# A 512-wide gate projection, weights outermost, in a two-layer hybrid block on one core

## The chip, the core and the metric

The kernel runs on one core of one Trainium2 chip. The metric is the device time of one execution in microseconds (us). The engines are named as in the profile: PE (matmuls; PEld are its weight loads), DVE (vector), ACT (activations and copies), POOL, and SP, whose queue here only issues DMAs. Each engine works through its own instruction list strictly in order, so an instruction that waits holds everything behind it on that engine.

## The reference

Two layers over 512 latent tokens (of width 1024) and 256 context tokens. Cut to what matters here:

```
for i in range(DEPTH):                       # 2 layers
    ctx_out = i < DEPTH - 1                  # the last layer gives no context output
    h  = rms_norm(x,  w) * (1 + sc_m)  + sh_m
    hc = rms_norm(cx, w) * (1 + csc_m) + csh_m
    ua, ub, ug = jnp.split(h @ w_in[i], splits, axis=-1)     # NA | SSD | GQA
    ...
    ya = neighbourhood_attention(...); yb = ssd_mixer(...); yg = gqa_attention(...)
    x = x + g_m * (concat([ya, yb, yg]) @ w_out[i])
    x = x + g_f * swiglu(...)

# in ssd_mixer: ub holds z (512 columns), xbc (1024 columns) and dt
z, xbc, dt_raw = jnp.split(v, [SSD_WIDTH, SSD_WIDTH + SSD_CONV_CH], axis=-1)
xbc = silu(depthwise_conv(xbc, conv_w, conv_b))
...
y = (y_f + flip(y_b) + d_skip * xs) * silu(z)                # the gate
y = rms_norm(y, norm_w)
```

The change concerns only `z`, the 512 columns of the input projection that gate the SSD output.

## The kernel before

Products are made from two parts, a rounded high part and a remainder, so each block of 128 rows of a projection takes three matmuls (high by high, high by low, low by high). Normed activations lie in SBUF as eight tiles of 128 features by 768 tokens, high parts `hh` and low parts `hl` (the names HY, HS, HZ, PHA, PHB in the profile). Tokens are counted in blocks of 128: `ntt` is 6 in layer 0 (latent and context) and 4 in layer 1 (latent only).

A layer runs through: norm, NA projections and attention, GQA projections, the eight blocks b of the SSD's `xbc` (projection on PE, a copy out of PSUM on ACT at L758 and L761, the convolution as a chain on DVE at L763 and L768, the tanh on ACT at L772, the product on DVE at L774), the decays of the SSD (L850: small products of `dA`; L852: ACT copies one to an SA tile, from which DMAs write `crow`), the z projection, and then the GQA or NA attention with the SSD core woven in between. The attention is cut into units: `scores` (PE L390 and L393 into a PSUM tile S, DVE L398 to L403 for the maximum, ACT L410 for the exponential, tile pr), then a scaling on POOL (L415), transposes (PE L424 into PSUM tiles PT, copies at L428 and L430) and the product with the values (PE L436). The SSD core's `diag` takes a chunk of tokens and four heads: it loads rows of `crow` into tiles wh and wl (L884, on SP's queue), then ACT L888 (four instructions), DVE L892 (four), ACT L894, a small matmul L897, DVE L899 and L900 into tiles SA and SB, POOL L903 into a tile MA, and DVE L907 and L908.

PSUM has three kinds of tile, two buffers of each: S of 1024 columns (two banks), PT and sm of 512 columns (one bank). In SBUF there are two buffers of SA (256 columns), two of MA (776 columns), two of `wr` for raw weights and three each of `wh` and `wl`, which `load_w` fills (DMA, ACT copy at L326, DVE subtraction at L327) and in which `diag` keeps its tiles too.

In the z projection `p_z(g)` works on one half g of the columns at a time. Two weight tiles, of four k each, are loaded; for each block of tokens 24 matmuls of 128x256 (in `proj_as`, activations stationary) fill one PT or sm tile, which is then read by ACT (L805, a tanh into an SA tile) and DVE (L806), and a DMA on ACT's queue (L807) writes the SA tile to a DRAM tile `zsp[g]`. `load_z` (L991, SP's queue) reads it back later into HZ tiles. The calls that come last put `scores(0)` and `scores(1)` of the first units between the last blocks of tokens.

The order of each engine is set once, when the kernel is built: a scheduler reads the program and fixes the lists. A tile's next user waits until every reader of the buffer before it is done.

## Time and profile before

| | |
|---|---|
| median of three runs | 1846.74 us (1846.3 to 1852.83) |
| profiled execution, span from first to last instruction | 1843.3 us |
| mean granted TensorE clock in it | 0.973 of full speed |
| PE busy | 1737.0 us (94%) |
| DVE, ACT, POOL busy | 1104.0 us (60%), 681.5 us (37%), 423.1 us (23%) |
| z projection in layer 0, first to last matmul | 258.36 us to 301 us of the span |
| z projection in layer 1 | 1265.53 us to 1291 us |

The profiled execution has no time of its own beside its span; the median of the runs lies 3.4 us above the span, and what lies around the first and the last instruction is in that difference. A share of busy time is a mean over stages; what ends last at a place is read from the waits and from the rows around it.

### The profile page before, as it was taken

Reading aid. Unit: us, or ns where it says so; the run is one execution under the profiler, and the core shown is the slowest. Engines: PE = TensorE matmul, PEld = TensorE weight load, DVE = VectorE, ACT = ScalarE, POOL = GpSimd, SP = SyncE. Lnnn points to the kernel's source line nnn. Section 1 sums busy time; section 2 is a strip of 40 time slices with the busy share of each in tenths; the row PEclk is TensorE's granted clock in tenths of the full one; section 3 lists DMA queues with packets and bytes.
Section 4 is the critical chain, followed back from the end, with each engine's and each line's share of the span. In section 5 each row is a group of like instructions: output and inputs, shape, how many; then the busy total and the mean of one; then the engine's idle time right before and its main releaser. Section 6 shows DMA issues by size and latency. Waiting matters only on the chain.

```text
span 1843.3 us, 26677 instructions
## 1 busy us (share of the span) xinstructions
PE 1737.0 (94%) x10146; PEld 1478.4 (80%) x10146; DVE 1104.0 (60%) x2209; ACT 681.5 (37%) x1386; POOL 423.1 (23%) x429
## 2 busy tenths in 40 slices
PE   7987778989999999999999999999899999999998
PEld 3887667777878888888888887989677788888887
DVE  4559996877475555455654576587786743333334
ACT  5554555556344221121112224334555442232222
POOL 0488886654010000000000002241653100000000
PEclk9998889989989999999999999999999999999999
DMA  9542526433123334333443454342631323333332
GB/s 368 201 139 103 163 89 186 140 90 106 56 75 115 114 115 126 103 116 107 124 129 102 130 163 139 96 131 79 183 105 53 108 90 93 99 96 92 103 100 83
DMA packets 94319, 221.66 MB, mean 120 GB/s; under 512 B 18416, under 2 KB 26224, under 8 KB 94192
## 3 DMA queue, kind: packets, MB, share of 16 engines
q1 hardware_dynamic: 78096, 204.65, 35.6%
q10 hardware_dynamic: 16096, 15.31, 2.5%
q8 instruction: 80, 1.31, 0.3%
q14 instruction: 47, 0.39, 0.1%
HBM read 198.49 MB, written 21.43 MB: 119 GB/s over the span
## 4 chain that ended last, share of the span: by engine, by line
PE 76%; DVE 11%; DMA 5%; ACT 3%; issue 2%; POOL 2%; SPq 0%; ACTq 0%; DVEq 0%; POOLq 0%
PE S L338 61%; PE sm L436 3%; DVE MB L768 2%; DMA wl<-crow 2%; PE PT L424 2%; DVE wl L327 1%; PE PT L338 1%; PE PT L352 1%; PE sm L352 1%; DMA wr<-in_mod_wT_dram 1%; DVE wh L892 1%; PE S L390 1%; ACT wh L326 1%; PE sm L913 1%; PE sm L914 1%
## 5 line engine op out<-in xcount | busy, mean ns | idle before, releaser
L326 ACT ACTIVATE wh<-wr 128x1024 fp32r<-128x1024 f32 (+3 forms) x214 | 207.6, 972 | 732.2 <-PE S L338 542.4
L327 DVE TENSOR_TENSOR wl<-wr,wh 128x1024 fp32r<-128x1024 f32 (+3 forms) x214 | 250.0, 1169 | 174.0 <-ACT wh L326 171.6
L269 POOL TENSOR_TENSOR tiny<-tiny,mhalf 128x2 f32<-128x2 f32 (+2 forms) x17 | 28.7, 1688 | 1067.5 <-DVE tiny L1160 1020.3
L338 PE MATMUL S<-HY,wh 128*128 128x512 f32 (+1 forms) x716 | 214.0, 357 | 5.9 <-ACT HY L318 4.1
L338 PE MATMUL S<-HY,wl 128*128 128x512 f32 (+1 forms) x716 | 214.5, 357 | 0.0
L338 PE MATMUL S<-HZ,wh 128*128 128x512 f32 (+1 forms) x716 | 212.8, 355 | 0.8 <-DVE HZ L319 0.8
L338 PE MATMUL S<-HS,wl 128*128 128x512 f32 (+1 forms) x716 | 213.1, 355 | 0.0
L338 PE MATMUL S<-HS,wh 128*128 128x512 f32 (+1 forms) x716 | 211.1, 353 | 0.0
L231 DVE CUSTOM_DVE_ANT_0 PT<-wr,XFB 128x512 f32<-128x512 f32 x112 | 75.5, 715 | 179.8 <-DMA wr<-in_mod_wT_dram 179.8
L338 PEld LDWEIGHTS S<-HY,wh 128*128 128x128 f32 x716 | 119.8, 192 | 27.2 <-ACT HY L318 4.4
L338 PEld LDWEIGHTS S<-HZ,wh 128*128 128x128 f32 x716 | 118.2, 191 | 21.7 <-DVE HZ L319 2.2
L338 PEld LDWEIGHTS S<-HS,wh 128*128 128x128 f32 x716 | 118.8, 191 | 20.2
L338 PEld LDWEIGHTS S<-HY,wl 128*128 128x128 f32 x716 | 118.8, 191 | 18.8
L338 PEld LDWEIGHTS S<-HS,wl 128*128 128x128 f32 x716 | 118.0, 190 | 18.6
L338 PE MATMUL S<-PHA,wh 128*128 128x512 f32 (+1 forms) x358 | 106.4, 355 | 0.0
L338 PE MATMUL S<-PHB,wh 128*128 128x512 f32 (+1 forms) x358 | 105.0, 351 | 0.0
L338 PE MATMUL S<-GX,wh 128*128 128x512 f32 (+1 forms) x400 | 97.2, 349 | 0.4 <-DVE KA L1114 0.4
L415 POOL TENSOR_SCALAR pr<-pr,tiny 128x640 f32<-128x640 f32 (+2 forms) x80 | 69.3, 869 | 84.0 <-DVE tiny L414 64.3
L768 DVE SCALAR_TENSOR_TENSOR MB<-MA,c,MB 128x770 f32<-128x770 f32 (+1 forms) x64 | 85.3, 1333 | 1.4
L228 POOL TENSOR_TENSOR KA<-QN,XFB 128x512 f32<-128x512 f32 x48 | 73.9, 1546 | 44.3 <-ACT XFB L205 23.5
L424 PE MATMUL PT<-c,pr 128*128 128x128 f32 x384 | 66.5, 289 | 13.4 <-POOL pr L415 4.6
L1261 DVE TENSOR_TENSOR MB<-S,MA 128x768 f32<-128x768 f32 (+1 forms) x42 | 34.6, 823 | 72.6 <-PE S L338 72.5
(402 smaller groups left out, 3911.7 us busy)
## 6 DMA issues: line engine op xcount, KB each, us to landing
wr<-in_mod_wT_dram SPq DMA_DIRECT2D x56, 512.0 KB, 3.7
wr<-in_w_gate_dram SPq DMA_DIRECT2D x44, 512.0 KB, 3.5
wr<-in_w_up_dram SPq DMA_DIRECT2D x44, 512.0 KB, 3.5
wr<-in_w_blk_dram SPq DMA_DIRECT2D x28, 512.0 KB, 3.6
wr<-in_w_down_dram SPq DMA_DIRECT2D x32, 448.0 KB, 3.3
QN<-in_mod_wT_dram SPq DMA_DIRECT2D x48, 256.0 KB, 3.3
wr<-in_w_out_dram SPq DMA_DIRECT2D x32, 256.0 KB, 2.6
wr<-in_w_down_dram SPq DMA_DIRECT2D x16, 512.0 KB, 3.4
```

The lines of the kernel that those rows point to most:

```text
L228: G.tensor_tensor(out=p_, in0=wv, in1=x, op=ALU.mult)
L231: V.tensor_tensor_reduce(out=p_, in0=wv, in1=x, scale=1.0, scalar=0.0, op0=ALU.mult, op1=ALU.add, accum_out=acc[:, o : o + 1],)
L269: POW.tensor_tensor(out=y, in0=v, in1=mhalf[:, 0:n], op=ALU.pow)
L326: S.activation(hi, raw, AF.Copy)
L327: V.tensor_tensor(lo, raw, hi.bitcast(F32), ALU.subtract)
L338: ins = PE.matmul(pt[:, c0:c1], lhsT=w, rhs=xx[:, c0:c1], start=(k == (0 if len(order) == 1 else order[0]) and i == 0), stop=(k == (nk - 1 ...
L352: PE.matmul(pt[:, 0:n], lhsT=s, rhs=w[:, o : o + n], start=(k == 0 and i == 0), stop=(k == KB - 1 and i == 2),)
L415: G.tensor_scalar(out=p_, in0=p_, scalar1=m[:, 4:5], scalar2=1.0, op0=ALU.mult, op1=ALU.mult)
L424: PE.transpose(pt[:, k * P : (k + 1) * P], pr[j, qi][:, kk * P : (kk + 1) * P], ident)
L436: PE.matmul(pv[64 * j : 64 * j + 64, 0:P], lhsT=V2(kts[k], j), rhs=ph[j, qi][:, k, :], start=(k == 0), stop=(k == nkt - 1), tile_position= ...
L768: V.scalar_tensor_tensor(ac[:, 0:wid], cp[:, j : j + wid], convw[l][:, b, j : j + 1], ac[:, 0:wid], ALU.mult, ALU.add)
L1261: V.tensor_tensor(gg[:, c0:c1], pu[:, c0:c1], sg[:, c0:c1], ALU.mult)
```

## The change

`p_z` no longer takes a half at a time. It takes a PSUM bank of 512 columns for every block of tokens at once: the two S tiles give four banks in layer 0 (in layer 1 one S tile gives two), and the last two blocks take the two PT tiles. The weights are regrouped: each of the four loads holds two k of all 512 columns. One load after the other passes by all blocks of tokens: six matmuls of 128x512 for each block and load, with `start` at the first k and `stop` at the last. Only in the fourth pass does a bank become complete; then ACT (L819) writes the tanh of 512 columns into an MA tile (before: 256 columns into SA), DVE (L820) makes the product and a DMA on ACT's queue (L821) writes it to the one DRAM tile `zsp`. `load_z` reads 256 of 512 columns of it, for three blocks of tokens at a time.

In numbers: 288 matmuls of 128x256 in layer 0 become 144 of 128x512, and 192 become 96 in layer 1. The tanh, the product and the DMA are issued 10 times instead of 20. The weight loads stay four in each layer, of the same size. Lines after the edit stand 14 lower than before (L888 becomes L902, L894 L908, L899 L913, L907 L921, L884 L898).

```
-        zsp = [dr.tile([P, 6, 256], F32, name=nm("zsp"), tag=nm("zsp")) for _ in range(2)]
-
-        def p_z(g):
-            wz = [load_w(a["w_z"][l, g, i].rearrange("p k c -> p (k c)"), 1024) for i in range(2)]
-            for t in range(ntt):
-                yield
-                pt = ps_sm() if t % 2 else ps_t()
-                proj_as(pt, wz, 256, 4, hh, hl, t)
-                th = sa()
-                S.activation(th, pt[:, 0:256], AF.Tanh, scale=0.5)
-                V.scalar_tensor_tensor(th, th, 1.0, pt[:, 0:256], ALU.add, ALU.mult)
-                nc.scalar.dma_start(zsp[g][:, t, :], th)
+        zsp = dr.tile([P, 6, 512], F32, name=nm("zsp"), tag=nm("zsp"))
+
+        def p_z():
+            pz = []
+            for t in range(0, ntt - 2, 2):
+                pt = ps_s()
+                pz += [pt[:, 0:512], pt[:, 512:1024]]
+            pz += [ps_t(), ps_t()]
+            for i in range(4):
+                wh, wl = load_w(a["w_z"][l, i].rearrange("p k c -> p (k c)"), 1024)
+                for t in range(ntt):
+                    yield
+                    for k in range(2 * i, 2 * i + 2):
+                        o = slice((k % 2) * 512, (k % 2) * 512 + 512)
+                        h0, l0 = (z[k][:, t * P : (t + 1) * P] for z in (hh, hl))
+                        for j, (s_, w) in enumerate(((h0, wh), (h0, wl), (l0, wh))):
+                            PE.matmul(
+                                pz[t], lhsT=s_, rhs=w[:, o],
+                                start=(k == 0 and j == 0), stop=(k == KB - 1 and j == 2),
+                            )
+                    if i == 3:
+                        th = ma([P, 512])
+                        S.activation(th, pz[t], AF.Tanh, scale=0.5)
+                        V.scalar_tensor_tensor(th, th, 1.0, pz[t], ALU.add, ALU.mult)
+                        nc.scalar.dma_start(zsp[:, t, :], th)
...
-                    nc.sync.dma_start(t[:, 0:n, :], zsp[g][:, 3 * i : 3 * i + n, :])
+                    nc.sync.dma_start(t[:, 0:n, :], zsp[:, 3 * i : 3 * i + n, 256 * g : 256 * g + 256])
...
-        for n, _ in enumerate(z for g in range(2) for z in p_z(g)):
-            if n == 2 * ntt - 2:
+        for n, _ in enumerate(p_z()):
+            if n == 4 * ntt - 2:
                 scores(0)
-            if n == 2 * ntt - 1:
+            if n == 4 * ntt - 1:
                 scores(1)
...
-    r["w_z"] = c(np.stack([act(wi[:, :, 768:1024]), act(wi[:, :, 1024:1280])], 1))
+    r["w_z"] = c(wi[:, :, 768:1280].reshape(2, 4, 2, 128, 512).transpose(0, 1, 3, 2, 4))
```

Three places show how the lists of the engines move. The first is PE's list at the end of z in layer 0, before: the last block of tokens (sm_2924) stands right ahead of `scores(2)`, the third unit.

```order
L352 MATMUL sm_2924<-wh_2729,HS_424 128x256
L352 MATMUL sm_2924<-wl_2730,HS_424 128x256
L352 MATMUL sm_2924<-wh_2729,PHB_432 128x256
L390 MATMUL S_2977<-KA_2861,QN_2858 128x384
L393 MATMUL S_2977<-KA_2861,QN_2858 128x256
L390 MATMUL S_2977<-KB_2864,QN_2858 128x384
L393 MATMUL S_2977<-KB_2864,QN_2858 128x256
L424 MATMUL PT_2999<-c_66,pr_2880 128x128 x3
```

The same place in the changed kernel: S_2534 holds blocks 0 and 1 of z, S_2535 blocks 2 and 3; S_2728 and S_2753 are the tiles of `scores(0)` and `scores(1)`.

```order
L813 MATMUL S_2534<-wl_2667,HS_424 128x512
L813 MATMUL S_2534<-wh_2666,PHB_432 128x512
L390 MATMUL S_2728<-KA_2713,QN_2710 128x384
L393 MATMUL S_2728<-KA_2713,QN_2710 128x256
L390 MATMUL S_2728<-KB_2716,QN_2710 128x384
L393 MATMUL S_2728<-KB_2716,QN_2710 128x256
L813 MATMUL S_2535<-wh_2666,HS_423 128x512
...
L813 MATMUL S_2535<-wh_2666,PHB_432 128x512
L390 MATMUL S_2753<-KA_2713,QN_2710 128x384
```

The scores now stand between the last blocks of z in the same two buffers of S: the first takes the buffer of blocks 0 and 1, the second that of blocks 2 and 3, so each has to wait until both of its banks have been read out.

The second place is ACT's list there, before: the tanh of a 256-wide block (L805), its DMA (L807) and the exponentials (L410) of the first two units alternate.

```order
L410 ACTIVATE pr_2880,tiny_2872<-S_2867,tiny_2872 128x640
L805 ACTIVATE SA_2907<-PT_2882 128x256
L807 DMA zsp_1197<-SA_2907 128x256
L410 ACTIVATE pr_2920,tiny_2916<-S_2911,tiny_2916 128x640
L805 ACTIVATE SA_2949<-sm_2924 128x256
```

In the changed kernel, from the eviction of block 0 (MA_2676) to the second exponential (pr_2762):

```order
L819 ACTIVATE MA_2676<-S_2534 128x512
L902 ACTIVATE wl_2921<-wl_2921,dtr_2519 128x128 x4
L821 DMA zsp_1196<-MA_2676 128x512
...
L819 ACTIVATE MA_2686<-S_2534 128x512
L819 ACTIVATE MA_2696<-S_2535 128x512
...
L819 ACTIVATE MA_2706<-S_2535 128x512
L410 ACTIVATE pr_2741,tiny_2733<-S_2728,tiny_2733 128x640
...
L819 ACTIVATE MA_2772<-PT_2537 128x512
L908 ACTIVATE wh_3058<-wh_3058 128x512
L410 ACTIVATE pr_2762,tiny_2758<-S_2753,tiny_2758 128x640
```

All six evictions now stand in a row through two buffers of MA, so each of them from the third on waits for the DMA of the one two before; the second exponential stands behind the sixth, and four instructions of `diag` (L902) stand between the first eviction and its DMA.

The third place is PE's list at the end of z in layer 1, where S_11573 holds blocks 0 and 1, and the other S buffer is free for the units; S_11778 is the tile of `scores(2)`. Before, `scores(2)` stood behind the last z matmul:

```order
L352 MATMUL sm_12024<-wl_11888,HS_10206 128x256
L352 MATMUL sm_12024<-wh_11887,PHB_10214 128x256
L390 MATMUL S_12073<-KA_11961,QN_11958 128x384
L393 MATMUL S_12073<-KA_11961,QN_11958 128x256
L390 MATMUL S_12073<-KB_11964,QN_11958 128x384
```

Now block 1 of z stands behind it:

```order
L813 MATMUL PT_11575<-wh_11668,PHB_10037 128x512
L390 MATMUL S_11778<-KA_11704,QN_11701 128x384
...
L393 MATMUL S_11778<-KB_11707,QN_11701 128x256
L813 MATMUL S_11573<-wh_11668,HS_10028 128x512
...
L813 MATMUL S_11573<-wh_11668,PHB_10037 128x512
L390 MATMUL S_11812<-KA_11704,QN_11701 128x384
```

The first two `scores` have moved up into the z projection there, the third stands before its last six matmuls.

## Rows read from the trace of the kernel before

**Rows 1.** The page, chain that ended last, share of the span by engine.

```profile
PE 76%; DVE 11%; DMA 5%; ACT 3%; issue 2%; POOL 2%; SPq 0%; ACTq 0%; DVEq 0%; POOLq 0%
```

**Rows 2.** Waits of PE, 258 to 330 us: in total, times, longest.

```profile
PE S L390 <- ACT pr L410: 6.5, 2, 6.2
PE PT L352 <- ACT SA L852: 4.3, 1, 4.3
```

**Rows 3.** Windows: PE, PEld, DVE, ACT, POOL busy; granted clock, DMA share, GB/s.

```profile
258.00:280.00 22.00, 17.73 (x127) 17.49 (x126) 19.98 (x19) 10.10 (x27) 18.95 (x13) 0.84 0.26 83
...
300.00:320.00 20.00, 11.77 (x62) 9.59 (x60) 15.84 (x45) 10.18 (x28) 15.63 (x22) 0.83 0.65 204
```

**Rows 4.** Timeline of PE, layer 0: start, duration, [idle before <- releaser].

```profile
258.36 0.28 PE L352 MATMUL sm<-wh,HY 128*128 128x256 f32 x1
...
264.42 0.28 PE L352 MATMUL sm<-wh,PHB 128*128 128x256 f32 x1
268.97 0.58 PE L352 MATMUL PT<-wh,HY 128*128 128x256 f32 x1 [4.27 <-ACT SA L852]
269.35 0.42 PE L352 MATMUL PT<-wl,HY 128*128 128x256 f32 x1
...
274.26 0.41 PE L352 MATMUL sm<-wh,HY 128*128 128x256 f32 x1
```

**Rows 5.** Timeline of ACT, layer 0, around the first stall.

```profile
265.50 0.84 ACT L772 ACTIVATE MA<-MB 128x770 f32<-128x770 f32 x1 [8.52 <-DVE MB L768]
...
268.28 0.37 ACT L761 ACTIVATE MA<-S 128x256 f32<-128x256 f32 x1
268.55 0.37 ACT L852 ACTIVATE SA<-PT 96x256 f32<-96x256 f32 x1
```

**Rows 6.** Timeline of PE, layer 0: `scores(2)` after z, and `scores(4)` after the second stall.

```profile
301.48 0.34 PE L390 MATMUL S<-KA,QN 128*128 128x384 f32 x1
...
310.47 0.69 PE L390 MATMUL S<-KA,QN 128*128 128x384 f32 x1 [6.20 <-ACT pr L410]
```

**Rows 7.** Timeline of DVE, layer 0, in the second stall.

```profile
307.19 0.29 DVE L899 TENSOR_TENSOR SA<-sm,c 128x128 f32<-128x128 f32 x1 [2.66 <-DMA zsp<-SA]
...
308.40 0.97 DVE L907 TENSOR_TENSOR wl<-wh,SB 128x512 f32<-128x512 f32 x1
...
309.75 0.67 DVE L908 TENSOR_TENSOR wh<-wh,SA 128x512 f32<-128x512 f32 x1
```

**Rows 8.** Timeline of SP's queue, layer 0, around the loads of z.

```profile
299.15 1.95 SPq L991 DMA_DIRECT2D HZ<-zsp  x3
...
307.17 0.33 SPq L884 DMA_DIRECT2D wh<-crow  x1
```

**Rows 9.** Waits of PE, 1265 to 1320 us.

```profile
PE S L390 <- ACT pr L410: 3.1, 2, 2.0
```

**Rows 10.** Timeline of PE, layer 1: a block of z, 24 matmuls, then scores.

```profile
1284.45 0.28 PE L352 MATMUL PT<-wh,HY 128*128 128x256 f32 x1
...
1287.33 0.34 PE L390 MATMUL S<-KA,QN 128*128 128x384 f32 x1
```

**Rows 11.** Timeline of PE, layer 1: 512-wide matmuls, six from the first to the last.

```profile
1255.51 0.40 PE L338 MATMUL S<-HZ,wh 128*128 128x512 f32 x1
...
1256.88 0.39 PE L338 MATMUL S<-PHA,wh 128*128 128x512 f32 x1
```

**Rows 12.** Timeline of ACT, layer 0: an exponential and the four instructions of diag.

```profile
309.53 0.79 ACT L410 ACTIVATE pr<-S,tiny 128x640 f32<-128x640 f32 x1 [5.88 <-DVE tiny L403]
...
310.32 1.27 ACT L888 ACTIVATE wl<-wl,dtr 128x128 f32<-128x128 f32 x4
```

**Rows 13.** Groups of DVE, 258 to 500 us: count | busy, mean ns of one.

```profile
L774 DVE SCALAR_TENSOR_TENSOR GC<-MA,MB 128x512 f32<-128x512 f32 x2 | 1.5, 744 | 1.4 <-ACT MA L772 1.4
```

**Rows 14.** Line L807, the DMA of z.

```profile
DMA to landing us min/median/max: 1.7/3.0/6.2
```

**Rows 15.** The page, DMA issues: count, KB each, us to landing.

```profile
wl<-crow SPq DMA_DIRECT2D x20, 256.0 KB, 4.0
```

## The prediction

> **What bounds the kernel now.** I read the chain that ended last first: three quarters of it are PE's own work, the rest is other engines and DMAs on which PE waited [rows 1]. So a change pays in two ways: by fewer PE cycles where PE runs without a gap, or by a shorter wait where it stands still. The table of PE's waits around the z projection of layer 0 shows where it stands still: two stalls, one of 4.3 us inside z and one of 6.2 us right behind it [rows 2]. The windows show what each stall costs beyond itself: the granted clock of the 20 us windows around them is 0.84 and 0.83 [rows 3]. The timeline has the same in single rows: after the first stall the 256-wide matmuls start 0.213 us apart (23 of them from 269.35 to 274.26) [rows 4], where they start 0.120 us apart in layer 1 (24 in 2.88 us) [rows 10]; that is 1.2 in place of 2.4 GHz, and 26 matmuls at 0.093 us more make 2.4 us.
>
> The first stall comes from ACT's queue. The next z matmul needs the PT buffer that the copy L852 reads; L852 stands behind a tanh of the convolution that waited 8.52 us for DVE's chain and began at 265.50, and behind the copies of the last `xbc` block, L761 among them [rows 5]. The second stall is longer: `scores(2)` ran right behind the last z matmul at 301.48, `scores(3)` passed too, and `scores(4)` at 310.47 waits for an exponential [rows 6], which itself sat behind a maximum on DVE, and DVE's queue stood at L899, whose SA buffer a z DMA was still reading [rows 7]. SP's queue was held too: it stood at the loads of z until 299.15, and the `crow` rows of the second and third `diag` could only be issued behind them, the last of these at 307.17 [rows 8]. In layer 1 the z projection has no stall of this kind; behind it PE waits 3.1 us in two pieces for exponentials [rows 9].
>
> **What the change does to PE's own time.** A 512-wide matmul takes 0.228 us from start to start (six in 1.37 us) [rows 11], two 256-wide ones 0.240 [rows 10]. Both are at the full clock and each has a weight load of its own, so the pair's saving is 0.012 us: 144 pairs in layer 0 make 1.7 us, 96 in layer 1 make 1.2 us, together **-2.9 us**. The bounds: none, if a 512-wide z matmul costs what two of 256 do, and -4 if the rounding of the rows (0.005 us a pair) falls the other way.
>
> The Trainium skill ("TensorE: Matmul & The Clock Gate", section "Wait — 56ns, not 53.3ns?") states a fixed cost of about 2.5 ns per matmul at the full clock on top of its columns. By that page alone a pair would give back 2.5 ns and the 240 pairs an estimated 0.6 us; the rows show 12 ns and are taken.
>
> **The first stall.** PE now does 30 matmuls of 512 (6.8 us) and the two small `dA` products (0.2 us) after its start at 258.36 before it needs something that is not free: the second S buffer, which ACT's L761 releases at 268.28 + 0.37 = 268.65. It stops at 265.4 and goes on at about 268.8, so it waits 3.4 us in place of 4.3: **-0.9 us**. The slow clock behind it stays, as the stop is of nearly the same length. Bounds: 0, if L852's copy, still one step later in ACT's list, is what is waited for, and -4.3 - 2.4 if ACT gets there early, for which nothing speaks, since the tanh that it waits for is DVE's and not touched. The first three passes have 78 matmuls left by then: 268.8 + 78 x 0.228 + 2.4 for the slow clock puts the start of the last pass at W = 289.0, and its 36 matmuls could end at 297.2 if nothing held them.
>
> **The end of z in layer 0.** This is the place where the change adds waits. Durations: tanh of 512 columns 0.6 (between a copy of 256 columns, 0.37 [rows 5], and an exponential of 640, 0.79 [rows 12]); product of 512 columns on DVE 0.74 [rows 13]; landing of a z DMA 3.0, at most 6.2 [rows 14]; `crow` rows 4.0 [rows 15]; the four ACT instructions of `diag` 1.27 [rows 12].
> - Block 0 is complete early in the pass. Its DMA on ACT's queue is behind `diag`'s four instructions, whose rows are loaded into a weight buffer that comes free at W: W + 0.5 + 4.0 + 1.3 = W + 5.8. It lands at W + 8.8 and frees the first MA buffer.
> - Block 1 is multiplied in order after blocks 0, 2, 4 and 5 and ends at W + 7.2. DVE reaches its product after work of `diag` at about W + 9.3 and is done at W + 10. `scores(0)` needs both banks of that buffer: it starts at W + 10.1, 2.9 us late.
> - Block 3 ends at W + 12.1. Its tanh waits for the DMA of block 1 (W + 13), the product ends at W + 14.4, and `scores(1)` starts there, 2.3 us late.
> - Block 5's tanh waits for the DMA of block 3: issued at W + 15, landed at W + 18. The second exponential stands behind it and ends at W + 20. So `scores(3)` runs at W + 20.2 = 309.2 and `scores(4)`, which needs the third exponential, at 310.0 to 311.
>
> Before, `scores(4)` ran at 310.47 [rows 6]. The 1.7 + 0.9 = 2.6 us by which z could end earlier are therefore eaten at this point: **+2.6 us**. Bounds: a single landing at 6.2 in place of 3.0 adds 3.2; if the `crow` rows come early, as their buffer is free in the pass before, 3 are saved.
>
> What comes back later: the `crow` rows of the second and third `diag` now stand ahead of the loads of z on SP's queue, and L899 no longer waits for a z DMA, since SA isn't used. The DVE work of `diag` which fell into the second stall and right behind it (L899, L907 and L908, 0.29 + 0.97 + 0.67 [rows 7], and some 1.5 that I reckon for L900 and L892 beside them) is done while PE waits for its evictions. That is some 3.4 us of DVE time out of the stretch in which each exponential waits for DVE. I take two thirds of it, **-2.2 us**, between 0 (another engine is late next: ACT, with as many instructions as before) and -3.4.
>
> **Layer 1.** Here one S buffer stays free, `scores(0)` and `scores(1)` move up into z, and the exponential of the first is done early. What is lost: `scores(2)` and then block 1 of z wait for exponential and eviction, and the second half of the units begins later by up to 4 us; what is gained are the two units that run under z. I take **0** between -3 and +3; PE's waits there are 3.1 us now [rows 9], so no more than that is to be had.
>
> **ACT and DVE counts.** 10 tanh of 512 in place of 20 of 256 save ACT 20 x 0.37 - 10 x 0.6 = 1.4 us [rows 5, 12], DVE saves something of the kind, and ten DMAs fewer are issued on ACT's queue. Both engines are half idle, so this counts at nothing. The loads of z read runs of 256 columns in place of whole rows; they are needed by the gate many units later, which hides them.
>
> **The sum.** -2.9 - 0.9 + 2.6 - 2.2 + 0 = -3.4 us. Against the profiled execution's span of 1843.3 that is 1839.9, and with the 3.4 us that lie between that span and the median, **1843**.
>
> **The rivals.**
> - *Nothing comes out* (a pair of 256 costs no more than one of 512, or what PE gains is waited away in both layers and stays away): -2.9 and -2.2 fall out, or the waits take them: 1845 to 1848. For it: `scores(4)` is at the same place by my own walk. Against: the rows on 512-wide matmuls.
> - *The second stall goes.* If the evictions keep pace (landings near 1.7 [rows 14], `crow` rows early), exponential two comes by 304, and PE neither stops for 6.2 us [rows 2] nor runs on at 1.2 GHz behind it. The clock of 0.83 over 20 us [rows 3] and a pause like that of the first stall put the slow piece at 2 to 2.5 us. -2.9 - 0.9 - 6.2 - 2.2 = -12: 1835. For it: the wait on SA is gone by construction. Against: the chain of three DMA round trips through two MA buffers.
> - *The banks are held* (slower). All S and both PT are full until the very end, and nothing can run on PE while ACT and DVE read them out. If the landings are at 6.2 twice in the chain of blocks 1, 3 and 5, `scores(4)` comes 6.4 us later; PE then has three stops in a row and starts each time at 1.2 GHz, some 2.4 us each for two of them [rows 4], and in layer 1, where block 1 and both PT banks are held in the same way, the bound of +3 is reached: -3.4 + 6.4 + 4.8 + 3 = +10.8, which is 1857.5. The point from which it decides: `scores(4)` later than some 316 in the new trace. The Trainium skill speaks for this side: "Perfetto Trace Analysis", section "Matmuls" under "Optimizing Tensor Performance", wants independent groups to rotate through different banks so that the read-out of one lies beside the matmuls of the next, and in the same place calls larger matmuls more efficient. The trace agrees with the first half: while z rotates through PT and sm in layer 1, no matmul of it waits. Against its weight here: only the last pass reads out, and PE has 36 matmuls to do meanwhile.
>
> **How the numbers follow.** The sum's case 0.52, with a range of its own of 1838 to 1848 from the bounds above; nothing comes out 0.19; the second stall goes 0.16; the banks are held 0.13. What a measurement of this kernel tells from no change is about 0.5%, 9.2 us. Only the third case is faster than that, with a little of the first: 0.17; only the fourth is slower: 0.13; the same 0.70. The range of 8 in 10 takes the first two cases whole and the near parts of the others: 1834 to 1854.
>
> **What the new profile would show.** z matmuls 0.228 us apart in both layers; the first stall at 265.4 for some 3.4 us, released by an ACT copy; a wait of 2 to 3 us ahead of `scores(0)` and of `scores(1)` in layer 0, named by DVE's product; the second exponential near 308 and behind L819; L899 without a wait for a z DMA; in layer 1 a wait ahead of `scores(2)`. Wrong I would be by the length of the eviction chain above all: by where the `diag` rows land on ACT's queue, and by what DVE does between the products.

## The result and the profile after

The changed kernel took **1861.32 us** in the median of four runs (1859.58 to 1864.02), the kernel before 1846.52 beside it on the same chip (1841.97 to 1852.83): a ratio of **1.0083, 95% interval 1.0065 to 1.0100**. It is slower by 15 us, outside the range of 1834 to 1854; the rival "the banks are held", 1857.5, came nearest. The profiled execution has a span of 1860.7 us and took 1862.52, so 1.8 us lie around a span and not 3.4; the mean granted clock is 0.965.

From the page of the changed kernel, the busy time of each engine, and the chain that ended last by engine (answers to [rows 1]):

```profile
PE 1743.2 (94%) x9906; PEld 1471.8 (79%) x9906; DVE 1102.2 (59%) x2199; ACT 681.8 (37%) x1376; POOL 419.3 (23%) x429
...
PE 77%; DVE 11%; DMA 7%; ACT 2%; issue 2%; POOL 1%; SPq 0%; ACTq 0%; DVEq 0%; POOLq 0%
```

PE is busy 6.2 us longer than before, though each z matmul is cheaper, and DMA has 7% of the chain in place of 5%. The waits of PE in layer 0 from 258 to 330 us (answers to [rows 2]):

```profile
PE S L813 <- ACT MA L761: 4.1, 1, 4.1
PE S L390 <- ACT pr L410: 4.1, 2, 2.6
PE S L390 <- DVE MA L820: 3.6, 1, 3.6
PE S L813 <- DVE MA L820: 2.0, 1, 2.0
PE PT L424 <- ACT PHA L428: 1.7, 1, 1.7
PE PT L424 <- POOL pr L415: 1.3, 1, 1.3
```

These are seven stops of 16.8 us in all. The one of 6.2 us is gone as one piece; waits for read-outs (DVE's L820), exponentials and copies stand in its place. The windows of the changed kernel (answers to [rows 3], and one in layer 1):

```profile
258.00:280.00 22.00, 17.91 (x72) 14.36 (x71) 17.82 (x15) 10.96 (x27) 14.71 (x11) 0.92 0.25 76
300.00:320.00 20.00, 11.53 (x41) 8.72 (x42) 11.26 (x35) 8.61 (x21) 6.37 (x9) 0.71 0.54 178
1305.00:1325.00 20.00, 14.24 (x60) 10.67 (x62) 13.58 (x34) 10.09 (x23) 9.61 (x12) 0.66 0.52 158
```

Around the first stall the clock is better than before, 0.92 for 0.84. Behind z it is worse, 0.71 for 0.83, with 41 matmuls in 20 us. The timeline of PE in the changed kernel, layer 0 (answers to [rows 4, 6]):

```profile
263.04 0.39 PE L813 MATMUL S<-wh,HZ 128*128 128x512 f32 x1
267.52 0.80 PE L813 MATMUL S<-wh,HY 128*128 128x512 f32 x1 [4.09 <-ACT MA L761]
...
271.88 0.39 PE L813 MATMUL PT<-wh,HY 128*128 128x512 f32 x1
...
286.84 0.39 PE L813 MATMUL S<-wh,HS 128*128 128x512 f32 x1
...
294.69 0.80 PE L813 MATMUL S<-wh,HS 128*128 128x512 f32 x1 [2.02 <-DVE MA L820]
...
301.24 0.48 PE L390 MATMUL S<-KA,QN 128*128 128x384 f32 x1 [3.63 <-DVE MA L820]
...
306.49 0.45 PE L390 MATMUL S<-KA,QN 128*128 128x384 f32 x1 [1.46 <-ACT pr L410]
...
313.42 0.69 PE L390 MATMUL S<-KA,QN 128*128 128x384 f32 x1 [2.59 <-ACT pr L410]
...
314.65 0.52 PE L390 MATMUL S<-KA,QN 128*128 128x384 f32 x1
...
317.22 1.33 PE L424 MATMUL PT<-c,pr 128*128 128x128 f32 x5 [1.30 <-POOL pr L415]
...
321.33 0.69 PE L390 MATMUL S<-KA,QN 128*128 128x384 f32 x1
```

The 66 matmuls from 271.88 to 286.84 are 0.227 us apart, as forecast, and the first stall has the releaser that it was given; it begins at 263.4 for a forecast of 265.4. The last pass began at W = 286.84. From there on all is later than the forecast: `scores(0)` (301.24) at W + 14.4 for W + 10.1, `scores(1)` (306.49) at W + 19.7 for W + 14.4, `scores(3)` (313.42) at W + 26.6 for W + 20.2. The stop at 294.69 had no place in the prediction at all: block 1 of z, in the second half of the S tile, waits until DVE has read block 0 out of the first half. The two pieces of SP's queue and of ACT's that set these times in the changed kernel:

```profile
286.80 5.81 SPq L358 DMA_DIRECT2D QN<-nq  x4
292.70 0.54 SPq L898 DMA_DIRECT2D wl<-crow  x1
...
304.63 0.32 SPq L898 DMA_DIRECT2D wl<-crow  x1
...
308.26 7.65 SPq L597 DMA_DIRECT2D GR<-in_rpb_dram  x3
```

```profile
296.86 0.40 ACT L902 ACTIVATE wl<-wl,dtr 128x128 f32<-128x128 f32 x1 [2.95 <-DMA wl<-crow]
296.87 0.33 ACTq L821 DMA_DIRECT2D zsp<-MA  x1
...
305.07 0.60 ACT L819 ACTIVATE MA<-S 128x512 f32<-128x512 f32 x1 [4.69 <-PE S L813]
...
311.32 0.60 ACT L819 ACTIVATE MA<-PT 128x512 f32<-128x512 f32 x1 [1.34 <-DMA zsp<-MA]
```

The `crow` rows of the second `diag` were not issued at W + 0.5 but at W + 5.9, behind four loads of `QN` that held SP's queue for 5.8 us. ACT therefore reached `diag`'s four instructions at 296.86, and the first DMA of z behind them left at W + 10.0 for W + 5.8. The rows of the third `diag` left at 304.63, behind z's last matmuls, whose weights are in the buffers that they go to; the `GR` rows stand behind them. POOL, in the changed kernel:

```profile
313.73 1.19 POOL L917 TENSOR_TENSOR MA<-GX,dtv 128x256 f32<-128x256 f32 x2 [6.19 <-DMA zsp<-MA]
...
316.37 1.57 POOL L415 TENSOR_SCALAR pr<-pr,tiny 128x640 f32<-128x640 f32 x2
```

The wait of L899 on SA [rows 7] is gone, as forecast. It has come back on MA: POOL's product for `diag` (L917) waits 6.2 us for a z DMA, and the scaling of the second exponential (L415) stands behind it. The transposes at 317.22 and `scores(5)` at 321.33 follow. In layer 1 the first two of these stops of PE were foreseen, the last two not (answers to [rows 9]):

```profile
1305.61 0.69 PE L390 MATMUL S<-KA,QN 128*128 128x384 f32 x1 [2.88 <-ACT pr L410]
...
1307.55 0.79 PE L813 MATMUL S<-wh,HS 128*128 128x512 f32 x1 [0.50 <-DVE MA L820]
...
1315.75 0.69 PE L424 MATMUL PT<-c,pr 128*128 128x128 f32 x2 [2.12 <-ACT PHA L428]
...
1318.88 0.87 PE L424 MATMUL PT<-c,pr 128*128 128x128 f32 x3 [1.82 <-DVE PHA L430]
```

**Where in the program the time lies.** I took three marks from the timeline of PE: z's first matmul, the last P V matmul (L436) of the layer, and z's first matmul of the next layer. From z to the last P V the profiled executions took

| | layer 0 | layer 1 |
|---|---|---|
| before, before again (e11), the old z beside a changed other layer (e2, e1) | 211.1, 210.4, 216.4 | 154.0, 153.7, 151.5 |
| after, after again (e5), the changed z in this layer alone (e1, e2) | 222.4, 219.4, 219.9 | 157.2, 160.1, 153.6 |

so the means are 8 us apart in layer 0 and 4 in layer 1, the single pairs 3 to 12 and 0 to 9. In layer 0 the three of a row have the same lists on PE, ACT and DVE, so the same lists spread over up to 6 us there from one execution to the next, and two single profiles do not show a smaller difference. Between the layers, from the last P V of layer 0 to z of layer 1, the changed kernel took 5.1 us more than before in its first profile and none more in e5: that was one execution's. Behind the last P V of layer 1 PE's remainder is 419 to 421 us in every profile. Inside layer 0, two pieces: the 60 us from z's start, and what follows. The changed kernel's windows for both, the second whole and then its first 100 us in three (the count behind PE's busy time is matmuls):

```profile
256.00:316.00 60.00, 44.42 (x179) 34.88 (x177) 38.34 (x61) 25.42 (x63) 33.54 (x34) 0.88 0.44 138
316.00:478.40 162.40, 148.60 (x1089) 119.27 (x1089) 117.50 (x333) 94.66 (x264) 88.45 (x113) 0.93 0.38 110
316.00:356.00 40.00, 35.32 (x246) 28.48 (x246) 23.51 (x72) 19.93 (x55) 25.96 (x33) 0.84 0.60 170
356.00:396.00 40.00, 34.83 (x255) 27.92 (x257) 32.89 (x96) 22.83 (x68) 25.08 (x34) 0.96 0.42 115
396.00:416.00 20.00, 17.70 (x112) 14.33 (x113) 15.99 (x43) 13.16 (x35) 8.50 (x11) 0.83 0.19 61
```

and the same two pieces, uncut, of the kernel before profiled again (e11), with a window of the feed-forward part as a third row, for the last section:

```profile
257.10:317.10 60.00, 48.11 (x346) 45.43 (x345) 42.65 (x76) 28.22 (x75) 43.59 (x42) 0.89 0.56 171
317.10:467.50 150.40, 138.07 (x1068) 111.30 (x1066) 114.96 (x325) 91.42 (x258) 81.94 (x105) 0.98 0.37 106
500.00:1000.00 500.00, 495.30 (x2852) 436.21 (x2851) 275.84 (x579) 119.73 (x145) 8.56 (x8) 0.99 0.37 113
```

A wide z matmul counts for two narrow ones, so the 346 of before are 202 of after (144 fewer); the changed kernel has done 179. The 23 that it lacks are, at before's 150.4 / 1068 = 0.141 us each, an estimated 3.2 us. The rest of the 12 us between these two profiles, 8.8 us, arises behind these 60 us (5 to 9 us over the pairs of before, e11, after and e5): the clock is 0.84, 0.96 and 0.83 in the next 100 us, and 0.98 over all that is left of the layer in e11. Part of this can come without the change: in e2, whose layer 0 is that of before, the same two pieces are

```profile
259.50:319.50 60.00, 45.59 (x336) 43.90 (x334) 39.51 (x70) 25.71 (x69) 39.92 (x39) 0.89 0.54 165
319.50:475.90 156.40, 142.71 (x1078) 114.66 (x1076) 118.74 (x331) 94.07 (x266) 84.79 (x108) 0.96 0.35 104
```

with 10 matmuls fewer than e11 in the first and 6.0 us more in the second.

### The profile page after: what moved, and what is told of

It is laid out like the page before. It is cut to its first block, busy times and chain, and to the rows that moved or that the text cites. A ratio compares the mean times of both kernels' runs of the same rounds, so it can differ in the third digit from the quotient of the medians.

```text
span 1860.7 us, 26142 instructions
## 1 busy us (share of the span) xinstructions
PE 1743.2 (94%) x9906; PEld 1471.8 (79%) x9906; DVE 1102.2 (59%) x2199; ACT 681.8 (37%) x1376; POOL 419.3 (23%) x429
## 4 chain that ended last, share of the span: by engine, by line
PE 77%; DVE 11%; DMA 7%; ACT 2%; issue 2%; POOL 1%; SPq 0%; ACTq 0%; DVEq 0%; POOLq 0%
PE S L338 59%; DMA wl<-crow 3%; PE sm L436 3%; DMA wr<-in_mod_wT_dram 2%; PE PT L424 2%; DVE MB L768 2%; DVE wl L327 2%; PE S L813 2%; PE PT L352 1%; PE PT L338 1%; PE S L390 1%; PE PT L813 1%; PE sm L352 1%; PE sm L927 1%; PE sm L928 1%
## 5 line engine op out<-in xcount | busy, mean ns | idle before, releaser
L326 ACT ACTIVATE wh<-wr 128x1024 fp32r<-128x1024 f32 (+3 forms) x214 | 207.7, 972 | 732.5 <-PE S L338 558.2
L415 POOL TENSOR_SCALAR pr<-pr,tiny 128x640 f32<-128x640 f32 (+2 forms) x80 | 68.3, 858 | 98.9 <-DVE tiny L414 77.4
```

What stands on the lines that cost most here:

```text
L326: S.activation(hi, raw, AF.Copy)
L415: G.tensor_scalar(out=p_, in0=p_, scalar1=m[:, 4:5], scalar2=1.0, op0=ALU.mult, op1=ALU.mult)
```

## The experiments

All ratios are to the kernel before, run in the same call, with 95% intervals. "L0" and "L1" are the two stretches of the table above. Diffs are against the changed kernel where nothing else is said. A profile is of one execution: those of e2, e4, e5 and e7 are of the longest of the kernel's runs, those of e3 and e16 of the shortest.

The lists are fixed anew for each kernel, so an edit also moves instructions that it does not name. I compared the order in the traces, from z's start to the last P V of layer 0 and without z's own instructions. Of 387 on DVE and 1121 on PE, so many stand outside the longest order that a kernel shares with the changed one:

| | DVE | PE |
|---|---|---|
| e7, e9 | 18, 25 | 29, 17 |
| before, e4, e8, e13 | 30, 30, 36, 41 | 24, 20, 41, 47 |
| e3 and e12, e6 and e14 | 95, 104 | 140, 142 |
| e16, e18 | 129, 148 | 257, 311 |

So the kernels of the last two rows differ from the changed one by another order as well as by their edit, and what they show is of both together.

**e1, e2: one layer alone.** The wide projection in one layer, the two halves of 256 in the other.

```diff
-        for n, _ in enumerate(p_z()):
+        wide = l in (0,)          # e2: (1,)
+        for n, _ in enumerate(p_z() if wide else (z for g in range(2) for z in p_zg(g))):
```

> The changed z projection in layer 0 alone, the old one in layer 1. Before 1846.5 us, changed kernel 1861.3. In the profile of the changed kernel the ACT weight copies run 1.2 us ahead of those of before when z of layer 0 begins, 8.9 late when its attention ends, 13 to 14 late in layer 1's start, 17.3 late at the end. If layer 0's z costs the 10 us and the steps of 5 us in between belong to the execution and not to the change: 1856 to 1858. If the 5 us follow the change in layer 0: 1860 to 1862. If both layers carry the loss alike: 1853 to 1855.

> The changed z projection in layer 1 alone. By the same reading of the ACT copies layer 1's z and attention lose 3.2 us: 1849 to 1851. If the loss of 5 us at the start of layer 1 belongs to the changed program of layer 1: 1853 to 1856. If layer 1 gains what its matmuls save: 1844 to 1846.

Layer 0 alone: 1852.61 us, 1.0030 [1.0018, 1.0042], L0 219.9. Layer 1 alone: 1845.49 us, 1.0001 [0.9978, 1.0024], L1 153.6, no longer than before. So layer 0 carries the loss, but the two parts, 7 and 0 us, do not add to the 13 to 15 of both: the 3 to 6 us of layer 1 only show where layer 0 is changed too. That stays open. The layer 0 of e2, which is that of before, is the 216.4 of the table.

**e3, e12: the width undone.** The same passes and the same banks, each 512 as two of 256 (`start` with the first half, `stop` with the second).

```diff
-  PE.matmul(pz[t], lhsT=s_, rhs=w[:, o], start=..., stop=...)
+  for q in (0, 256):
+      PE.matmul(pz[t][:, q : q + 256], lhsT=s_, rhs=w[:, o][:, q : q + 256], start=..., stop=...)
```

> The changed kernel with each 512-wide z matmul as two of 256 into the same bank; weights outermost, banks, evictions and order of passes as changed. If the waits at the end of z carry the loss and the width only the -2.9 us that the rows gave: 1862 to 1865. If the width itself is what costs: 1847 to 1852. If the width gains nothing because the end of z is set by waits on DMAs that do not move: 1861 again.

> The kernel with each z matmul as two of 256 once more, a second profile. In the first one layer 0's feed-forward part, which no edit touches, took 580.5 us where all other kernels take 589 to 590. If that belongs to the program, it shows again and the kernel's 1846.2 hides a loss of some 9 us in the attention; if it was one execution's, the part takes 589 to 590.

1846.20 us, 1.0003 [0.9988, 1.0018]: with dearer matmuls the loss is gone (e12 is one profiled execution, 1852.13). L0 is 214.9 and 212.3. By the time alone that is the case "the width itself is what costs", but 95 of 387 DVE instructions stand elsewhere too, so the width is not shown to be the cause. The timeline of PE in e3 shows that block 1 no longer stops:

```profile
297.74 0.50 PE L814 MATMUL S<-wh,HS 128*128 128x256 f32 x2
...
301.24 0.41 PE L390 MATMUL S<-KA,QN 128*128 128x384 f32 x1 [1.22 <-issue]
```

PE comes to block 1 at 297.74 without a stop, and `scores(0)` runs at 301.24, 43.2 us after z's start (45.3 in the changed kernel). PE arrives later, waits less, and gets its scores no later: up to there, what the 512 columns save is waited away.

**e4: diag behind z.** A DVE instruction that adds nothing to `ncum` but reads the last product of z, so that `diag`'s work on ACT and DVE in layer 0 stands behind all read-outs.

```diff
                         nc.scalar.dma_start(zsp[:, t, :], th)
+                        if t == ntt - 1 and l == 0:
+                            V.scalar_tensor_tensor(fl(ncum), th[:, 0:96], 0.0, fl(ncum), ALU.mult, ALU.add)
```

> The changed kernel, with one DVE instruction more in layer 0, which adds zero times the last block's product to the tile ncum that all of diag's first steps read: no ACT or DVE instruction of diag can stand ahead of z's evictions any more. Queue theory (evictions wait on ACT and DVE behind diag's instructions, which wait for their crow rows): the waits of PE ahead of block 1, scores(0) and scores(1) in layer 0, 2.0 + 3.6 + 1.5 us, shrink to 2 to 3 in all, and the slow clock around them with them: 1853 to 1857. Buffer theory (two MA buffers, each freed by a DMA): the waits stay, 1860 to 1863. If diag itself, now later, becomes what attention waits for: 1860 or more with the waits of PE moved to scores(4) and behind.

1856.55 us, 1.0063 [1.0031, 1.0094]. `scores(0)` comes at 37.6 us after z's start, nearly 8 us earlier, as the theory of ACT's queue has it; the stops ahead of block 1, `scores(0)` and `scores(1)` are 0.5, 1.4 and 1.5 us for 2.0, 3.6 and 1.5, with one of 2.2 us ahead of block 3 beside them, and the time is in that theory's range. Yet L0 is still 216.9, and the interval overlaps that of the changed kernel: the scores at the right time bring back a small part at most.

**e5, e6, e7: the changed kernel again, the read-out in pairs, more buffers.** e5 is the changed kernel itself. In e6 the two blocks of an S tile are read out together after the second, so that block 1 needn't wait for block 0's read-out; in e7 z's products go through four tiles.

```diff
-                    if i == 3:
-                        th = ma([P, 512])
+                    # e6, with e in place of t below
+                    for e in (([t - 1, t] if t % 2 else []) if t < ntt - 2 else [t]) if i == 3 else []:
+                        th = ma([P, 512])
+                    # e7
+                        th = (ma, ma, lambda s: T(sb, "ZT", 1, s), mc, ma, ma)[t]([P, 512])
```

> The changed kernel once more, beside the three that follow. So far its layer-0 stretch from z's first matmul to the last P V of the attention took 222.4 us (219.9 in the kernel with layer 0 alone changed; 211.1 and 216.4 in two with the old layer 0), and the stretch from the last blocks of layer 0's w_down to layer 1's z 4.7 us more than before (209.5 against 204.8; 208.6 in the kernel with diag behind z). If both belong to the program: 1859 to 1863, with 220 or more and 208 or more in those stretches. If the second is a matter of one execution's DMA landings: 1853 to 1858 and 205.

> The changed kernel, but blocks that share an S tile (0 and 1, 2 and 3) are read out one after the other behind the second of them, so that the matmuls of block 1 (3) no longer wait until block 0 (2) has been read. Theory of the shared tile: the wait of 2.0 us ahead of block 1 goes, scores(0) and scores(1) come earlier by it, the slow clock begins later: 1856 to 1859. Queue theory (ACT and DVE stand at diag's instructions): block 1's matmuls run early, but scores(0) waits as long as before for the read-out: within 2 us of the changed kernel. Buffer theory: no change.

> The changed kernel with the products of blocks 0 to 3 in four different SBUF buffers (two of MA, one new, one of MC) in place of two, so that only blocks 4 and 5 wait for a DMA of another block. Buffer theory: the second exponential comes 2 to 5 us earlier, 1855 to 1858. Queue theory: ACT waits only 2.4 us for those DMAs in the changed kernel, so no more than 2 us come back: 1859 to 1862.

e5: 1856.83 us, 1.0081 [1.0051, 1.0111], the result again. e6: 1849.69 us, 1.0034 [1.0014, 1.0055]. Its timeline of PE has one long stop ahead of `scores(0)` where the changed kernel has two:

```profile
294.64 0.38 PE L911 MATMUL sm<-GC,GT 128*128 128x128 f32 x2
301.63 0.69 PE L390 MATMUL S<-KA,QN 128*128 128x384 f32 x1 [6.61 <-DVE MA L820]
```

Another of 2.7 us follows ahead of `scores(1)`. `scores(0)` is only 1.9 us earlier after z's start (43.4), but L0 is 210.9 (and L1 158.3). e7: 1845.60 us, 1.0009 [0.9989, 1.0030], with L0 217.1 and L1 151.7. So over half of the loss goes with the first edit and nearly all with the second, and their profiles put it in different layers; but the execution of e7 that was profiled took 1852.73, 7 us over the median, so it does not show where the median's gain lies.

**e8, e9, e14: combinations.** e8 has pairs, four buffers and e4's instruction, e9 pairs and four buffers, e14 pairs in layer 0 and four buffers in layer 1.

> Pairs read out together, four buffers, and diag's first steps in layer 0 behind z's last block. If the layer-0 loss is the read-out chain in any of its three forms, the stretch from z's first matmul to the last P V falls to 212 to 216 us: 1850 to 1855. If what is lost lies in diag's lateness or in the fact that all banks come free at one time, it stays at 217 or more: 1856 or above.

> Pairs read out together and four buffers, diag where the scheduler puts it. Reading out pairs brought layer 0's stretch from 219 to 222 us down to 210.9, but left layer 1's at 158.3; four buffers brought layer 1's from 157 to 160 down to 151.7 and left layer 0's at 217.1. If each cures the layer that it cured alone: 211 and 152, 1841 to 1846, level with the kernel before or a little under it by what the 240 wider matmuls save (2.9 us). If the two cures stand in each other's way, as in the kernel with all three: 1847 to 1850.

> The changed kernel with the read-out in pairs in layer 0 alone (the two blocks of an S tile after the second one) and the four buffers for z's products in layer 1 alone: in each layer the edit whose profile had the shorter stretch (210.9 us in layer 0 with pairs, 151.7 us in layer 1 with four buffers). If the stretches are what the time is made of, they come out again and add to 1843 to 1846, a little under the kernel before or level with it; if they were one execution's chance, the time is between those of the two edits alone, or above: 1846 to 1850.

e8: 1849.01 us, 1.0032 [1.0007, 1.0058], L0 211.0, L1 154.0. e9: 1846.16 us, 0.9994 [0.9978, 1.0011], L0 211.7, L1 157.2. e14: 1846.89 us, 1.0008 [0.9988, 1.0029], L0 210.7, L1 154.9. The loss is recovered, the 2.9 us of PE time are not seen in any of them. e9 is the one to read: with nearly the order of the changed kernel (25 of 388 instructions moved on DVE, 17 of 1122 on PE) and all six banks full until the last pass, it is level with the kernel before. Its first 60 us have 190 matmuls for 179, and what follows takes 151.7 us, at a clock of 0.97, for 162.4 at 0.93. The 151.7 of layer 1 did not come again in e14: a single profile's stretch is good to some 3 us in layer 1 and, by the table above, to some 6 in layer 0.

**e10, e15: the kernel before with tiles of its own for z's products.** Diff against the kernel before:

```diff
-                th = sa()
+                th = T(sb, "ZA", 3, [P, 256])
                 S.activation(th, pt[:, 0:256], AF.Tanh, scale=0.5)
```

> The kernel before with one edit: the products of z go to three tiles of their own in place of the two SA tiles that diag uses as well. If the second stall of layer 0 (6.2 us, behind a DVE instruction of diag that waits for a z DMA to leave its SA tile) is worth what it lasts, its slow clock with it: 1838 to 1842. If what comes next in that queue (the exponentials, diag's own loads of crow, issued behind the loads of z) is as late: 1844 to 1847.

> The kernel before with z's products in three tiles of their own, run and profiled again: the first time it was 0.27% faster than the kernel before, and its profile did not show where. If that is the wait of DVE on the SA buffers that is gone, it is 1840 to 1843 again, and the stretch of layer 0 from z's start to the last P V is 1 to 4 us below that of the kernel before; if it was chance, it lies within 0.15% of the kernel before.

1841.49 us, 0.9973 [0.9957, 0.9988], and again 1840.79 us, 0.9989 [0.9970, 1.0008]. L899's wait on SA is gone without a wide z, and the second stall of PE is 3.2 us in both profiles for 6.2 [rows 2]. This is the fastest of all versions; that it is faster than before is clear in one call and not in the other, and L0 (213.2 and 210.3) doesn't show where.

**e11: the kernel before, profiled again.**

> The kernel before, a second profile. Layer 0's stretch from z's first matmul to the last P V was 211.1 us in the first profile, 216.4 in the kernel that changes layer 1 alone. If 211 is the program's value, the changed kernel loses 8 to 11 us there; if 216 is, it loses 3 to 6 and the rest of the 15 has to be found elsewhere.

One execution, 1834.61 us. Its L0 and L1 are in the table above; what made it 12 us shorter lies mostly elsewhere, in the feed-forward part, and is told at the end.

**e13: POOL's wait alone.** `diag`'s products on POOL go into a tile of their own.

```diff
-            xfb = ma([P, 2, 4, 64])
+            xfb = T(sb, "ZT", 1, [P, 2, 4, 64])
```

> The changed kernel with one edit: diag's products on POOL (L917) go into a tile of their own (one buffer of 512 elements per partition) in place of the two MA buffers that z's products use. Theory A (the wait of POOL for a z DMA, which holds the scaling of the second exponential and so scores(5), is what the long end of layer 0 is made of): no wait of POOL on MA behind z, scores(5) at some 55 us after z's first matmul in place of 65 to 66, the stretch from z's start to the last P V of layer 0 near 212 us in place of 219 to 222, and a time of 1848 to 1852. Theory B (the read-out of six full blocks ahead of the scores is the cost, the wait on POOL lies beside it): scores(0) at 45 us after z's start as before the edit, the stretch stays at 217 or more, and the time stays at 1855 to 1861.

1855.31 us, 1.0064 [1.0043, 1.0084], L0 217.2, `scores(5)` at 62.3 us after z's start. By the numbers that is theory B, but the timeline of POOL in e13 shows that the run did not take POOL's wait away:

```profile
311.89 1.52 POOL L598 TENSOR_TENSOR GR<-GR,c 128x768 f32<-128x768 f32 x1 [6.89 <-DMA GR<-in_rpb_dram]
313.39 1.58 POOL L415 TENSOR_SCALAR pr<-pr,tiny 128x640 f32<-128x640 f32 x2
```

POOL now waits 6.9 us for the `GR` rows, ahead of the same L415. Those rows stand behind the third `diag`'s `crow` rows on SP's queue (issued from 302.10) and then waited another 2.6 us, until 306.1, for a maximum on DVE (L398). So what POOL's wait is worth stays open.

**e16, e17, e18: diag's list two units later.** In the changed kernel (e16), in the kernel before (e17), and in e9's kernel (e18).

```diff
-UCFG = [(0, 42, 0.5, 44, 22, 46, 47, 48), (0, 28, 0.5, 30, 0, 31, 32, 33)]
+UCFG = [(2, 44, 0.5, 44, 22, 46, 47, 48), (0, 28, 0.5, 30, 0, 31, 32, 33)]
```

> The changed kernel with the list of diag's steps in layer 0 shifted by two units (from units 0 to 42 to units 2 to 44), so that the crow rows of the first diag are issued behind two units' worth of other work, and none of its ACT, DVE and POOL work stands between the products of z. Theory C (diag's work in the six full banks' read-out, and the crow rows that hold SP's queue until z's last matmul, so that the GR rows and z's loads behind them come late, are the loss): no wait of POOL ahead of the second exponential's scaling for a z DMA or a late GR load, scores(0) at 37 to 38 us after z's start, scores(5) at 55 to 58 us, the stretch of layer 0 at 210 to 214 us, and a time of 1845 to 1850. Theory D (diag's work is only moved and is missed later, as when it stood behind z by a wait): scores(0) early, the stretch at 216 or more, 1853 to 1858.

> The kernel before with the same shift of diag by two units: what the shift is worth where z is projected 256 columns wide. Theory C: the exponential behind z no longer waits for a product of diag on SA, so 0 to 4 us less than before (1841 to 1846). Theory D: 3 to 6 us more (1848 to 1852), as diag's work is missed at the end of its list.

> The changed kernel with the read-out in pairs, the four buffers for z's products, and diag two units later. Theory C: the 2.9 us of PE time come out at last, 1840 to 1844, under the kernel before. Theory D: level with the version without the shift or above it, 1846 to 1851.

e16: 1849.91 us, **1.0018** [1.0005, 1.0031]. e17: 1848.63 us, 1.0020 [1.0003, 1.0037], L0 215.7. e18: 1850.35 us, 1.0021 [1.0007, 1.0035], L0 216.9; these two are theory D. With this list the wide and the narrow z are level, and the shift that costs the kernel before 3 to 4 us gives the changed one 9 to 12. But not as theory C has it. `scores(0)` comes at 43.1 us and `scores(5)` at 63.3 us after z's start, and ACT's rows still have the first `diag`s between the read-outs: the steps of the first three `diag`s stand in ACT's and SP's order where they stood, and only the later ones have moved. The end of z is as bad as in the changed kernel. The windows of e16 show what is different (the same cut as for the changed kernel):

```profile
255.40:315.40 60.00, 45.77 (x182) 35.80 (x180) 38.16 (x62) 25.72 (x64) 35.94 (x37) 0.85 0.48 147
315.40:355.40 40.00, 37.62 (x282) 30.47 (x282) 29.40 (x95) 24.21 (x68) 29.83 (x36) 0.96 0.59 166
355.40:395.40 40.00, 36.06 (x274) 28.80 (x272) 35.21 (x97) 26.34 (x77) 24.47 (x34) 1.00 0.42 109
395.40:415.40 20.00, 18.59 (x157) 14.82 (x157) 14.71 (x43) 10.83 (x30) 10.12 (x14) 1.00 0.30 87
```

182 matmuls for 179 in the first 60 us; in the next 100 us 282 + 274 + 157 = 713 for 613, at granted clocks of 0.96, 1.00 and 1.00 for 0.84, 0.96 and 0.83. L0 is 211.4. The profiled execution took 1843.6, the shortest of 12, so some of its 211.4 may be luck; the median of the 12 says that not all of it is. In e6 and e12 the stretch behind the first 60 us has a clock of 0.99 too (150.9 and 152.3 us), in e1 and e5 of 0.95 (159.9 and 159.4 us).

## Why the prediction was wrong

- **PE's own time: right.** 0.227 us a matmul for 0.228 forecast, and e3 has pairs at 0.240 in the same place. The sum's -2.9 is there as work saved and nowhere as time: no version with the wide z is clearly faster than before.
- **The first stall: right in place and releaser, 4.1 us for 3.4.** PE came to it 2.0 us earlier than forecast, since z began at 255.96 and not at 258.36, and waited until 267.5 for a forecast of 268.8: the term is -0.2 and not -0.9. The slow clock behind it lasted some 3 us (0.43 us from start to start).
- **The end of z in layer 0: right as a mechanism, mis-sized.** The walk put the `diag` rows that z's first DMA stands behind on ACT at W + 4.5 and they were there at W + 10.0, because I had taken SP's queue for free; and it had block 1 run through while block 0 is read out of the other half of its tile, which costs 2.0 us. The rows forecast as waits (DVE's product ahead of `scores(0)`, a wait ahead of `scores(1)`) are there. The term was +2.6 against 1.7 + 0.9 gained, so level; the 23 missing matmuls make it an estimated +3.2 net, and the term 5 to 6.
- **What comes back later, -2.2: the step that failed.** It had the wrong sign. `diag`'s products did leave L899's queue, but POOL's took over the wait on a z DMA and held the scaling of the second exponential. Behind the first 60 us the layer takes 162.4 and 159.4 us in the changed kernel (after, e5) for 151.1 and 150.4 (before, e11), at clocks of 0.93 and 0.95 for 0.97 and 0.98, so 8 to 12 us more in place of 2.2 less; an estimated 3.2 of them are the matmuls not done by then, and 5 to 9 are this term. What makes them stays open. It is not tied to when the scores begin (e4: early, L0 long; e16: late, L0 short), and e13 could not tell what POOL's wait adds. Two things took it away: another order of the lists (e16, and with their edits e3 and e6), and the read-out in pairs through four buffers at nearly the same order (e9). And e2 has 156.4 us in this piece with the old z, so up to 6 us of it can be an execution's own; that layer 0 loses by the change rests on the median of e1, 7 us.
- **Layer 1, 0 between -3 and +3: at its upper bound or over it**, +3 to +6 in the profiles of the whole change against before and e11, and 0 in e2. The wait ahead of `scores(2)` is there as forecast (2.9 us); the two waits at the transposes, 2.1 and 1.8, were not.
- **The rival.** "The banks are held" gave 1857.5 and came nearest. Its sign to watch, `scores(4)` later than 316, was wrong: it ran at 314.65. Later by the yardstick of z's start it was, 58.7 us for 52.1. That it came near in time is in part luck. Its place was too narrow: it put all of the loss into the end of z, and the larger part lies behind it. And in e9 all six banks fill up over the four passes in the same way, at no loss, so holding them is not by itself what costs. The Trainium skill ("Perfetto Trace Analysis", "Matmuls" under "Optimizing Tensor Performance") asks for groups that rotate through different banks, so that one is read out beside the matmuls of the next. In this trace each block has a bank of its own, and block 1 waits 2.0 us at 294.69 all the same, for the read-out of the block in the other bank of its tile: here it is the tile that has to rotate. I gave this side 0.13 because no z matmul waited for a bank before the change; in the new order one waits for a tile.

## What to carry to other kernels

A cheaper matmul ahead of a fixed chain of read-outs can buy a wait: before a width saving is counted, walk the chain that releases the next stage, with every load that stands ahead on the same DMA queue. Where the work beside a stage comes from an order written as numbers, price the change with that order shifted a little both ways: here the same shift cost one kernel 3 to 4 us and gave the other 9 to 12, most of what the change had cost. Where a scheduler fixes the lists, compare them before a run is read as the effect of its edit: e3 was meant to undo the width alone, and moved a quarter of DVE's instructions in layer 0 too. And a stretch's own mark (matmuls done by then, granted clock behind it) tells more than the time of one instruction: `scores(5)` was 8 to 9 us later in e16 than before the change, and the layer ended on time.

## What the runs showed that I had not expected

- **A feed-forward part with two rates.** The third row of e11 above has 2852 matmuls in 500 us; the changed kernel has, in the same window,

```profile
500.00:1000.00 500.00, 495.62 (x2798) 430.35 (x2797) 273.12 (x568) 117.87 (x144) 8.56 (x8) 0.99 0.36 110
```

  Granted clock 0.99 and PE busy 495 of 500 us in both, and 1.9% fewer; the first profile of the kernel before has 2800. From the first to the 78th weight copy on ACT (L326) behind layer 0's attention it is 579.5 us in e11 and 580.5 in e3, and 587 to 590 in every other profile, the first one of the kernel before included. None of the edits touches that part. It can be one cause of the spread of before's runs (1830.92 to 1853.12 over all calls); what sets it I don't know.
- **Longer stops at z's end, and a shorter layer.** e6 stops for 6.6 and 2.7 us ahead of `scores(0)` and `scores(1)`, the changed kernel for 2.0, 3.6 and 1.5; L0 is 210.9 in the one and 219 to 222 in the other. What follows runs at 0.99 in e6 and at 0.93 and 0.95 in the changed kernel (after, e5). That the stops as such make this clock is not shown, since e6 changes the order behind them too.
